# Packed first loads and a by-token last projection in a float32 decoder trunk

## Chip, core and metric
One NeuronCore of one Trainium2 chip runs the whole program in one launch. The metric is device time in microseconds (us) of one execution; the runs shown are separate executions of the same program. Engines are named as in the profile: PE (TensorE), PEld (its weight loads), DVE (VectorE), ACT (ScalarE), POOL (GpSimd), SP (the engine that issues most transfers).

## The reference, cut to what matters
A trunk of two pre-norm layers on x of shape (1, 256, 1024), all float32: `h = h + mixer(rmsnorm(h))`, `h = h + conv_ffn(rmsnorm(h))`, twice, then a final norm.

```python
z = h @ w_in                       # conv_ffn: 1024 -> 2 * 2816
u, g = z[..., :D_FF], z[..., D_FF:]
a = causal_dwconv(u, conv_w) + conv_b
return (silu(a) * g) @ w_out       # 2816 -> 1024
...
return rmsnorm(h, final_norm_g)    # h * rsqrt(mean(h * h) + 1e-6) * g
```

The mixer of layer 0 starts with one input projection `hn @ w_in` of 2048 columns, cut by channel into a double-gated convolution and a pooling path. Layer 1 has attention heads instead.

## The kernel before, in words
P is 128, T is 256 tokens, D is 1024, and NK = 8 chunks of 128 channels. The residual `h` lives in SBUF by channel: `h[128, 8, 256]`. Every matmul operand is split into a high and a low float32r part, and every product is three matmuls (`mm3`, L272 to L275): high by high, high by low, low by high. Weights stream from memory in blocks of 128 x 1024 floats (rows of 4 KB; 512 KB a block). A block is loaded on SP's queue (L139), ACT casts it to its high part (L131), DVE subtracts to get the low part (L132), and up to six blocks are prepared ahead (`ahead`). The order of PE's instructions is the program order; the other engines are ordered by a scheduler, except in the stretches under `manual_schedule`, where ACT and DVE too keep the program order.

The start (L242 to L269): the first unit of layer 0 needs all of `h` and four blocks of weights (two of kind x, two of kind y). They come in five steps of chunks, (0,1), (1,2), (2,4), (4,6), (6,8). Each step issues three transfers on SP: its chunks of `h` (L252) and the matching columns of one x block and one y block (L254). Rows are 1 KB for the first two steps and 2 KB for the others. The norm's weights `vec[:, :8]` come by POOL's queue (L171). Then, step by step, ACT and DVE scale `h` by the norm weights and split it (`hgh`, `hgl`, L194 and L195) and cut the weights. PE runs 12 matmuls per chunk, 96 in all (L434 to L438). The token norm's factor is applied later, to rows of the results (`rrow`), so that the projection need not wait for it.

Layer 0's mixer goes on by units: pooling and convolution of a unit run on DVE, POOL and ACT while PE projects the next units; `even_add` then adds their output products, and `yb` (L394) is the pooling path's split input to them.

The MLP (`ffn`, L483): for each of 22 channel blocks f, an input step of 48 matmuls of 256 columns (`z`), and four blocks later an output step of 24 matmuls of 256 columns. `Acc` (L311) holds the output by channel: eight accumulators of 128 channels x 256 tokens in four PSUM banks. The weights are the stationary operand (128 x 128) and the hidden values `y` of 256 tokens the moving one. The last two blocks' products are kept as `tail`, and `close` (L329) runs them bank by bank and adds the residual on DVE (L337).

The end (`final`, L768): after the last MLP, `h` is by channel and the final norm is by token. So PE turns `h` in 16 transposes of 128 x 128 (L781), two per chunk, between the `close` steps and after the last; ACT sums the squares (L786); DVE works out the variance of both token blocks together, POOL raises it to the power of -0.5 (L806), and ACT and DVE scale the output (L810, L812), which leaves in five transfers on SP's queue (L811, L813).

Of the kernel before, what the change touches and what calls it, by code (L numbers as in the profile page):

```python
# [18 lines left out]
P = 128  # L19
# [21 lines left out]
LOOK = 6  # L41

# columns of the packed per-channel vectors
# [5 lines left out]
def trunk(ctx, tc, a, out):  # L49
# [35 lines left out]
    for j in range(NG):  # L85
        even_in_blocks(j)
        if j >= 2:
            even_out_blocks(j - 2)
# [82 lines left out]
    nc.gpsimd.dma_start(vec[:, :NK], a["vec"][:, :NK])  # L171
# [29 lines left out]
    class Stats:  # L201
        """The mean square of h per token, and from it the norm's factor, by column and by row."""
# [4 lines left out]
        def feed(self, b):  # L207
            """Squares of h's chunks 2b, 2b+1."""
# [38 lines left out]
    def step_parts(k0, k1):  # L247
        s, e = (k0 % 4) * 256, (k0 % 4 + k1 - k0) * 256
        return [(i, s, e) for i in (k0 // 4, 2 + k0 // 4)]
# [5 lines left out]
    for i in range(4):  # L255
        done[blocks[i][0]] = first[i][1:]
# [9 lines left out]
    state["next"] = 4  # L266
    ahead(6)
    nc.sync.dma_start(vec[:, NK:], a["vec"][:, NK:])
    nc.sync.dma_start(rc, a["rcnt"])  # L269

# [6 lines left out]
    def in_chunk(o, w, hg, between=None):  # L277
        """o[f, t] = sum_k w[k, f] hg[k, t]; between() comes halfway."""
# [6 lines left out]
    def in_pair(z, at, hg, between=None):  # L285
        """Two chunks that share a bank, in step; at(k, c) gives the weights of chunk c's rows k."""
# [7 lines left out]
    def split(pool_, src, scale, name, bufs=None, between=None):  # L294
        """src (SBUF or PSUM) times a per-partition scale, as two float32r parts."""
# [15 lines left out]
    class Acc:  # L311
        """Eight [128, 256] accumulators over four PSUM banks."""
# [15 lines left out]

    def close(acc, tail, b, between=None):  # L329
        """The last products of an output projection's bank b, and the residual."""  # L330
# [5 lines left out]
        hb = h[:, 2 * b:2 * b + 2, :]  # L336
        nc.vector.tensor_add(hb, acc.t[b], hb)  # L337

    def boundary(acc, tail, g0):
        """The end of an output projection, and the next layer's input."""  # L340
# [11 lines left out]
    # causal convolution over time, width 3, on the free axis: t = the newest tap, then the two before it  # L352
# [11 lines left out]

    with tc.tile_pool(name="ev", bufs=2) as ev, tc.tile_pool(name="evc", bufs=1) as evc:
# [5 lines left out]
        def pool_sums(j, z):  # L371
            """Trailing sums, by doubling."""
# [7 lines left out]
        def pool_less(j):  # L380
            """Trailing mean less the token."""
# [50 lines left out]
        w0 = [[weights(("e" + kind, 0, q)) for q in range(2)] for kind in "xy"]  # L432
        zx0, zy0 = (psA.tile([P, 2, T], F32, tag="ps", name="z" + kind) for kind in "xy")
        for k in range(NK):  # L434
            for c in range(4):
                wh, wl = (x[:, (k % 4) * 256 + (c % 2) * P:][:, :P] for x in w0[c // 2][k // 4])
                mm3((zx0, zy0)[c // 2][:, c % 2, :], wh, wl, hg[0][:, k, :], hg[1][:, k, :],
                    k == 0 and c % 2 == 0, k == NK - 1, skip=True)  # L438
        ahead()
# [40 lines left out]
        st, hg = boundary(acc, tail, V_FFN)  # L480

# [1 line left out]
    def ffn(l, st, hg, ps_z, ps_acc, end, aside=None):  # L483
        with tc.tile_pool(name=f"ff{l}", bufs=2) as fp:
            acc = Acc(ps_acc)
# [16 lines left out]
            for kind, f in ffn_steps:  # L502
                if kind == "out":
                    acc.add_all(weights(("fo", l, f)), ready.pop(f))
# [26 lines left out]
    # T5 bias along each query row, negated, with the causal mask beyond it  # L531
# [15 lines left out]
    st, hg = ffn(0, st, hg, psA, psB, lambda acc, tail: boundary(acc, tail, V_MIX + NK), t5_rows)  # L547

# [1 line left out]
    with tc.tile_pool(name="od", bufs=2) as od, tc.tile_pool(name="odc", bufs=1) as odc:  # L550
# [4 lines left out]
        def values(n):  # L555
            """Values by token, 512 channels."""
# [19 lines left out]
        # forget gates  # L576
# [34 lines left out]
        def pair_bias(p):  # L611
            """Forget sums of a FoX pair's keys, or the T5 biases of a MoBA pair's queries."""
# [276 lines left out]
```

## Time and profile before

| what | value |
|---|---|
| device time, three runs | 590.21, 590.57, 592.21 us; median 590.57 |
| profiled execution, first to last instruction (span) | 588.8 us |
| profiled execution's own device time | not listed apart from its span |
| PE busy | 575.7 us, 98% |
| DVE busy | 429.9 us, 73% |
| ACT busy | 324.9 us, 55% |
| POOL busy | 78.9 us, 13% |
| bytes moved by transfers | 106.07 MB, mean 180 GB/s |

The busy time of PE counts overlapping matmuls, whose ends are modelled; the pace of PE is read from the distance between starts. An engine's idle time matters only where the others wait for it.

### The profile page before, as it was taken

To read this page: it belongs to the slowest core of one execution; us is meant where nothing else is said; L and a number is where in the kernel's file an instruction comes from. 1 tells how busy PE (TensorE), PEld (TensorE's weight loads), DVE (VectorE), ACT (ScalarE), POOL (GpSimd) and SP (SyncE) were. 2 spreads that over 40 slices of the span, in tenths; PEclk is the share of its full clock that TensorE was granted. 3 is DMA by queue.
4 is the path that set the end of the run, shared out by engine and by line. 5 is a ranking of instruction groups with operands and counts; after the bars stand their busy time and mean duration, and the time that the engine had idled before them with its cause. 6 is when DMAs were issued, how large, how long until landed. Compare 5 with 4: busy or idle time off the path is not lost.

```text
span 588.8 us, 11640 instructions
## 1 busy us (share of the span) xinstructions
PE 575.7 (98%) x4664; PEld 562.8 (96%) x4664; DVE 429.9 (73%) x700; ACT 324.9 (55%) x538; POOL 78.9 (13%) x91
## 2 busy tenths in 40 slices
PE   8999999999999999999999999999999999999993
PEld 6999999999999999998898999999999999999993
DVE  5899687876568677668678888498767677766733
ACT  6764476554355454447577777476554444545412
POOL 1441231000000000004162164031000000000000
PEclk9999999999999999999999999999999999999997
DMA  8975726656687555653675534347555555554001
GB/s 250 401 269 190 241 81 245 215 171 132 151 320 235 184 189 185 188 180 129 215 218 178 162 127 145 126 143 249 187 190 184 185 187 180 180 181 141 1 1 71
DMA packets 31941, 106.07 MB, mean 180 GB/s; under 512 B 4256, under 2 KB 5416, under 8 KB 31888
## 3 DMA queue, kind: packets, MB, share of 16 engines
q1 hardware_dynamic: 30240, 101.09, 50.8%
q0 software_dynamic: 1648, 4.25, 4.2%
q8 instruction: 36, 0.59, 0.4%
q14 instruction: 17, 0.14, 0.1%
HBM read 102.69 MB, written 2.63 MB: 179 GB/s over the span
## 4 chain that ended last, share of the span: by engine, by line
PE 60%; issue 32%; DVE 4%; ACT 1%; DMA 1%; POOL 0%; SPq 0%; POOLq 0%; ACTq 0%
PE z L274 8%; PE z L273 7%; PE z L275 7%; PE acc L273 6%; PE acc L274 6%; PE acc L275 6%; PE zk L273 1%; DVE lo L132 1%; PE zq L273 1%; PE pv L565 1%; PE zk L274 1%; PE zk L275 1%; PE pv L567 1%; PE pv L566 1%; PE zq L274 1%
## 5 line engine op out<-in xcount | busy, mean ns | idle before, releaser
L132 DVE TENSOR_TENSOR lo<-st,hi 128x1024 fp32r<-128x1024 f32 (+2 forms) x196 | 235.3, 1210 | 85.1 <-ACT hi L131 84.9
L131 ACT CAST hi<-st 128x1024 fp32r<-128x1024 f32 (+2 forms) x196 | 196.7, 1012 | 154.6 <-PE z L274 62.3
L274 PE MATMUL z<-hgl,hi 128*128 128x256 f32 x704 | 199.6, 284 | 0.1
L273 PE MATMUL z<-hgh,hi 128*128 128x256 f32 x704 | 199.7, 284 | 0.0
L275 PE MATMUL z<-hgh,lo 128*128 128x256 f32 x704 | 199.5, 283 | 0.0
L274 PEld LDWEIGHTS z<-hgl,hi 128*128 128x128 f32 x704 | 135.0, 192 | 0.5 <-DVE hgl L195 0.5
L275 PEld LDWEIGHTS z<-hgh,lo 128*128 128x128 f32 x704 | 135.0, 192 | 0.0
L273 PEld LDWEIGHTS z<-hgh,hi 128*128 128x128 f32 x704 | 135.0, 192 | 0.0
L273 PE MATMUL acc<-y_h,hi 128*128 128x256 f32 x352 | 99.7, 283 | 0.0
L274 PE MATMUL acc<-y_l,hi 128*128 128x256 f32 x352 | 99.2, 282 | 0.0
L275 PE MATMUL acc<-y_h,lo 128*128 128x256 f32 x352 | 99.2, 282 | 0.0
L273 PEld LDWEIGHTS acc<-y_h,hi 128*128 128x128 f32 x352 | 66.5, 189 | 0.4 <-issue 0.4
L274 PEld LDWEIGHTS acc<-y_l,hi 128*128 128x128 f32 x352 | 66.4, 189 | 0.0
L275 PEld LDWEIGHTS acc<-y_h,lo 128*128 128x128 f32 x352 | 66.3, 188 | 0.0
L492 DVE TENSOR_TENSOR zs<-z,rrow 128x512 f32<-128x512 f32 x44 | 30.2, 690 | 19.9 <-PE z L275 19.7
L300 ACT CAST y_h<-y 128x256 fp32r<-128x256 f32 x44 | 17.9, 406 | 47.9 <-DVE y L499 47.9
L357 ACT ACTIVATE t<-zs,vec 128x256 f32<-128x256 f32 x44 | 26.3, 598 | 9.2 <-DVE zs L492 9.2
L306 DVE TENSOR_TENSOR y_l<-y,y_h 128x256 fp32r<-128x256 f32 x44 | 18.7, 424 | 16.5 <-ACT y_h L300 16.5
L215 POOL TENSOR_TENSOR sqs<-sq 128x512 f32<-128x512 f32 x4 | 5.2, 1295 | 186.4 <-ACT sq L210 161.9
L195 DVE SCALAR_TENSOR_TENSOR hgl<-h,vec,hgh 128x256 fp32r<-128x256 f32 x32 | 22.3, 735 | 6.8 <-ACT hgh L194 6.8
L806 POOL TENSOR_TENSOR rcol<-var,mhalf 128x2 f32<-128x2 f32 x1 | 0.7, 689 | 182.2 <-DVE var L804 182.2
L361 DVE SCALAR_TENSOR_TENSOR t<-zs,vec,t 128x254 f32<-128x254 f32 x44 | 21.2, 483 | 1.5
(197 smaller groups left out, 1002.6 us busy)
## 6 DMA issues: line engine op xcount, KB each, us to landing
st<-in_ff_in SPq DMA_DIRECT2D x88, 512.0 KB, 3.7
st<-in_ff_out SPq DMA_DIRECT2D x44, 512.0 KB, 3.3
st<-in_od_qk SPq DMA_DIRECT2D x16, 512.0 KB, 4.6
st<-in_ev_in SPq DMA_DIRECT2D x10, 512.0 KB, 7.7
st<-in_ev_out SPq DMA_DIRECT2D x8, 512.0 KB, 4.5
st<-in_od_v SPq DMA_DIRECT2D x8, 512.0 KB, 4.2
st<-in_od_out SPq DMA_DIRECT2D x8, 512.0 KB, 4.0
st<-in_ev_in SPq DMA_DIRECT2D x10, 256.0 KB, 5.5
```

The source lines that it names most:

```text
L131: nc.scalar.copy(hi[:, s:e], st[:, s:e])
L132: nc.vector.tensor_sub(lo[:, s:e], st[:, s:e], hi.bitcast(F32)[:, s:e])
L195: nc.vector.scalar_tensor_tensor(hg[1][:, k, :], h[:, k, :], g, hg[0].bitcast(F32)[:, k, :], op0=ALU.mult, op1=ALU.subtract)
L273: nc.tensor.matmul(o, wh, xh, start=start, stop=False, skip_group_check=skip)
L274: nc.tensor.matmul(o, wh, xl, start=False, stop=False, skip_group_check=skip)
L275: nc.tensor.matmul(o, wl, xh, start=False, stop=stop, skip_group_check=skip)
L300: nc.scalar.copy(hi, src)
L306: nc.vector.tensor_sub(lo, src, hi.bitcast(F32))
L357: nc.scalar.activation(t, u, AF.Identity, scale=col(w0 + 2), bias=bias)
L361: nc.vector.scalar_tensor_tensor(t[:, 2:], u[:, :T - 2], col(w0), t[:, 2:], op0=ALU.mult, op1=ALU.add)
L492: nc.vector.tensor_mul(zs, z, rrow[:, None, :].to_broadcast([P, 2, T]))
L565: nc.tensor.matmul(pv[i], xh, wh, start=k == 0, stop=False)
```

## The change
Two edits go together.

The start. The host lays the first unit's inputs out in one array `first` of 8 x 128 rows of 776 floats (3104 bytes): the norm weight of the row's channel, seven floats of padding, 256 tokens of x, and 512 weights of the four projections. It is loaded in nine transfers on SP, one per chunk, with the first chunk's in two. The four blocks no longer use the staging buffers. POOL's load of the norm weights goes; `vec` comes whole, on SP, after six blocks of weights. ACT and DVE cut chunk by chunk, in program order; the first chunk's high part is copied by DVE. PE takes the first chunk's products in another order. Layer 0's residual is read from `first`, and `h` is written for the first time at the end of layer 0's mixer.

The end. In the last MLP a new `TokenAcc` holds the output by token: four banks of 128 tokens x 512 channels. At its creation, which is now at the first output step, 16 transposes put `h` into the banks, and the products add to it: `y` of 128 tokens is the stationary operand and 512 weights the moving one, 12 matmuls of 512 columns per output step. `final` then finishes block of tokens by block of tokens; there are no residual adds and no transposes in it. Each block's first half is stored from ACT's queue, the second from SP's.

```diff
-        piece = 512 if i < 6 else BLK
+        piece = 512 if i < 2 else BLK
...
-    nc.gpsimd.dma_start(vec[:, :NK], a["vec"][:, :NK])
...
-    first = [block_tiles(i) for i in range(4)]
-    steps = [(0, 1), (1, 2), (2, 4), (4, 6), (6, 8)]
...
-    for k0, k1 in steps:
-        nc.sync.dma_start(h[:, k0:k1, :], a["xt"][:, k0:k1, :])
-        for i, s, e in step_parts(k0, k1):
-            nc.sync.dma_start(first[i][0][:, s:e], blocks[i][1][:, s:e])
+    first = fst.tile([P, NK, FIRST], F32, name="first")
+    w0h, w0l = ([wgt.tile([P, 2, 512], F32R, tag=t, name=f"{t}{m}_0") for m in range(4)] for t in ("hi", "lo"))
+    x0 = first[:, :, LEAD:LEAD + T]
+    w0 = first[:, :, LEAD + T:]
+    resid = {"t": x0}
+    for k in range(NK):
+        for s, e in ((0, LEAD + T), (LEAD + T, FIRST)) if k == 0 else ((0, FIRST),):
+            nc.sync.dma_start(first[:, k, s:e], a["first"][k, :, s:e])
     st = Stats()
     with tc.manual_schedule(engines={mybir.EngineType.Activation, mybir.EngineType.DVE}):
-        for k0, k1 in steps:
-            for k in range(k0, k1):
-                scaled_chunk(hg, k, V_MIX)
-            for i, s, e in step_parts(k0, k1):
-                cut(*first[i], s, e)
+        for k in range(NK):
+            g = first[:, k, 0:1]
+            nc.scalar.activation(hg[0][:, k, :], x0[:, k, :], AF.Copy, scale=g)
+            wh, wl = (t[k // 2][:, k % 2, :] for t in (w0h, w0l))
+            if k == 0:
+                nc.vector.tensor_copy(wh, w0[:, k, :])
+            else:
+                nc.scalar.copy(wh, w0[:, k, :])
+            nc.vector.scalar_tensor_tensor(hg[1][:, k, :], x0[:, k, :], g, hg[0].bitcast(F32)[:, k, :],
+                                           op0=ALU.mult, op1=ALU.subtract)
+            nc.vector.tensor_sub(wl, w0[:, k, :], w0h[k // 2].bitcast(F32)[:, k % 2, :])
         for b in range(4):
-            st.feed(b)
+            st.feed(b, x0)
     ahead(6)
-    nc.sync.dma_start(vec[:, NK:], a["vec"][:, NK:])
+    nc.sync.dma_start(vec, a["vec"])
...
+    class TokenAcc:
+        def __init__(self, ps):
+            self.t = [[ps.tile([P, 512], F32, tag="ps", name=f"ta{i}{n}") for n in range(2)] for i in range(2)]
+            for k in range(NK):
+                for i in range(2):
+                    nc.tensor.matmul(self.t[i][k // 4][:, (k % 4) * P:(k % 4 + 1) * P], h[:, k, i * P:(i + 1) * P],
+                                     ident, is_transpose=True, start=k % 4 == 0, stop=False, skip_group_check=True)
+
+        def add(self, i, n, w, y, last):
+            s = slice(n * 512, (n + 1) * 512)
+            yh, yl = (x[:, i * P:(i + 1) * P] for x in y)
+            mm3(self.t[i][n], yh, yl, w[0][:, s], w[1][:, s], False, last, skip=True)
...
+            products = [(w, x, c) for c in range(4) for w, x in ((w0h, 0), (w0h, 1), (w0l, 0))]
+            if k == 0:
+                products = [(w, x, c) for w, x in ((w0h, 0), (w0h, 1), (w0l, 0)) for c in range(4)]
...
             for i in range(2):
-                r = rcol[:, i:i + 1]
-                for lo, hi in ((0, 256), (256, 512)) if i == 0 else ((0, 512),):
-                    nc.scalar.activation(o[:, i, lo:hi], hg_[:, i, lo:hi], AF.Copy, scale=r)
-                    nc.sync.dma_start(out[i, :, lo:hi], o[:, i, lo:hi])
-                nc.vector.scalar_tensor_tensor(o[:, i, 512:], pt[i][1], r, gb[:, 512:], op0=ALU.mult, op1=ALU.mult)
+                r, v = rcol[:, i:i + 1], var[:, i:i + 1]
+                for n in range(2):
+                    for m, (w, y) in enumerate(tail):
+                        acc.add(i, n, w, y, m == len(tail) - 1)
+                    nc.scalar.activation(junk, acc.t[i][n], AF.Square, accum_out=sums[:, i, n:n + 1])
+                    if n == 0:
+                        nc.vector.tensor_mul(hg_[:, i, :], acc.t[i][0], gb[:, :512])
+                        nc.vector.tensor_scalar(v, sums[:, i, 0:1], 1.0 / D, EPS, op0=ALU.mult, op1=ALU.add)
+                nc.vector.scalar_tensor_tensor(v, sums[:, i, 1:2], 1.0 / D, v, op0=ALU.mult, op1=ALU.add)
+                nc.gpsimd.tensor_tensor(r, v, mhalf[:, 0:1], op=ALU.pow)
+                nc.vector.scalar_tensor_tensor(o[:, i, 512:], acc.t[i][1], r, gb[:, 512:], op0=ALU.mult, op1=ALU.mult)
+                nc.scalar.activation(o[:, i, :512], hg_[:, i, :], AF.Copy, scale=r)
+                nc.scalar.dma_start(out[i, :, :512], o[:, i, :512])
                 nc.sync.dma_start(out[i, :, 512:], o[:, i, 512:])
...
-    ffn(1, st, hg, psB, psA, ordered_final)
+    ffn(1, st, hg, psB, psA, TokenAcc, ordered_final)
```

## Rows read from the trace of the kernel before

**Rows 1.** The page's first part: busy time and share of the span.
```profile
span 588.8 us, 11640 instructions
PE 575.7 (98%) x4664; PEld 562.8 (96%) x4664; DVE 429.9 (73%) x700; ACT 324.9 (55%) x538; POOL 78.9 (13%) x91
```
**Rows 2.** Waits of PE, whole span: who waited for whom, total us, times, longest.
```profile
PE zx L273 <- ACT hi L131: 1.4, 1, 1.4
PE fin L781 <- DVE h L337: 0.9, 1, 0.9
PE acc L274 <- DVE ybl L308: 0.8, 1, 0.8
```
**Rows 3.** Windows of the start: length, PE, PEld, DVE, ACT, POOL busy, PEclk, DMA share, GB/s.
```profile
2.00:5.00 3.00, 3.00 (x8) 1.88 (x7) 0.40 (x1) 1.16 (x5) 1.21 (x4) 1.00 0.92 244
5.00:11.00 6.00, 4.36 (x28) 3.90 (x29) 3.79 (x10) 3.67 (x9) 0.00 (x0) 1.00 0.90 240
11.00:16.00 5.00, 5.00 (x44) 5.00 (x43) 4.45 (x9) 4.95 (x11) 0.15 (x1) 1.00 1.05 396
16.00:33.00 17.00, 17.00 (x144) 17.00 (x143) 15.65 (x21) 12.99 (x18) 9.62 (x9) 1.00 1.03 403
```
**Rows 4.** Timeline of the start: start, us, engine, line, op, out<-in [idle before <-releaser].
```profile
0.73 0.39 SPq L252 DMA_DIRECT2D h<-in_xt  x1
...
4.06 0.51 ACT L194 ACTIVATE hgh<-h,vec 128x256 fp32r<-128x256 f32 x1 [1.83 <-DMA vec<-in_vec]
...
4.91 0.58 PE L273 MATMUL zx<-hgh,hi 128*128 128x256 f32 x1
...
8.38 0.91 ACT L194 ACTIVATE hgh<-h,vec 128x256 fp32r<-128x256 f32 x2 [2.14 <-DMA h<-in_xt]
...
9.93 0.39 PE L273 MATMUL zx<-hgh,hi 128*128 128x256 f32 x1 [1.42 <-ACT hi L131]
...
14.18 1.29 DVE L132 TENSOR_TENSOR lo<-st,hi 128x512 fp32r<-128x512 f32 x2
...
19.16 0.28 PE L273 MATMUL zx<-hgh,hi 128*128 128x256 f32 x1
```
**Rows 5.** DMA issues of the first 30 us: size of each, median us to landing.
```profile
h<-in_xt SPq DMA_DIRECT2D x2, 128.0 KB, 2.6
```
**Rows 6.** DVE after the first unit (timeline), and the window of the first mixer.
```profile
16.30 1.99 DVE L132 TENSOR_TENSOR lo<-st,hi 128x512 fp32r<-128x512 f32 x2 [0.83 <-ACT hi L131]
...
26.00:66.00 40.00, 39.16 (x328) 38.96 (x327) 37.56 (x68) 21.65 (x31) 9.94 (x11) 1.00 0.72 254
```
**Rows 7.** Window of the last MLP, columns as in the windows above.
```profile
440.00:575.00 135.00, 135.00 (x1132) 135.00 (x1132) 87.77 (x120) 61.71 (x88) 0.00 (x0) 1.00 0.41 137
```
**Rows 8.** Timeline of one output step: its first product, and the next input step's.
```profile
503.31 0.28 PE L273 MATMUL acc<-y_h,hi 128*128 128x256 f32 x1
...
506.16 0.28 PE L273 MATMUL z<-hgh,hi 128*128 128x256 f32 x1
```
**Rows 9.** Timeline of layer 1's second values: first product, and what follows them.
```profile
290.99 0.40 PE L565 MATMUL pv<-hi,hgh 128*128 128x512 f32 x1
...
301.90 0.28 PE L273 MATMUL zq<-hgh,hi 128*128 128x256 f32 x1
```
**Rows 10.** Timeline of the end, from the first tail product to the last store.
```profile
572.10 0.28 PE L273 MATMUL acc<-y_h,hi 128*128 128x256 f32 x1
...
574.95 0.60 PE L781 MATMUL fin<-ident,h 128*128 128x128 f32 x4
...
576.80 0.60 PE L781 MATMUL fin<-ident,h 128*128 128x128 f32 x4
...
577.33 0.60 ACT L786 ACTIVATE junk<-fin 128x512 f32<-128x512 f32 x1 [9.80 <-PE fin L781]
...
581.82 0.69 POOL L806 TENSOR_TENSOR rcol<-var,mhalf 128x2 f32<-128x2 f32 x1 [182.18 <-DVE var L804]
...
582.54 1.41 DVE L812 SCALAR_TENSOR_TENSOR o<-fin,rcol,gb 128x512 f32<-128x512 f32 x2 [0.81 <-POOL rcol L806]
...
584.98 0.40 SPq L813 DMA_DIRECT2D out<-o  x1
```

More of the change, by code (lines that the diff above doesn't have):

```diff
@@ L41 @@
 LOOK = 6
+LEAD = 8
+FIRST = LEAD + T + 512
 V_MIX, V_FFN, V_FIN, V_EC, V_PS, V_FC, V_FB = 0, 16, 32, 40, 52, 56, 188
@@ L83, in even_out_blocks @@
         block(("eo", j + NG), a["ev_out"][GROUPS[j] + NG])
-    for j in range(NG):
+    for j in range(1, NG):
         even_in_blocks(j)
@@ L327, in add_all @@
                 self.add(dc, w, y, False)
+    class TokenAcc:
[9 more added lines that the diff above has]
+            mm3(self.t[i][n], yh, yl, w[0][:, s], w[1][:, s], False, last, skip=True)
+        def add_all(self, w, y):
+            for i in range(2):
+                for n in range(2):
+                    self.add(i, n, w, y, False)
     def close(acc, tail, b, between=None):
@@ L430, in even_in @@
             return z
-        w0 = [[weights(("e" + kind, 0, q)) for q in range(2)] for kind in "xy"]
         zx0, zy0 = (psA.tile([P, 2, T], F32, tag="ps", name="z" + kind) for kind in "xy")
         for k in range(NK):
[L435 to L439, printed above, removed]
+            products = [(w, x, c) for c in range(4) for w, x in ((w0h, 0), (w0h, 1), (w0l, 0))]
+            if k == 0:
+                products = [(w, x, c) for w, x in ((w0h, 0), (w0h, 1), (w0l, 0)) for c in range(4)]
+            for n, (w, x, c) in enumerate(products):
+                nc.tensor.matmul((zx0, zy0)[c // 2][:, c % 2, :], w[k // 2][:, k % 2, c * P:(c + 1) * P], hg[x][:, k, :],
+                                 start=k == 0 and w is w0h and x == 0 and c % 2 == 0,
+                                 stop=k == NK - 1 and w is w0l, skip_group_check=True)
         pwb = small_block(evc, a["ev_pw"], "pw")
@@ L480, in trunk, with ffn @@
         st, hg = boundary(acc, tail, V_FFN)
-    def ffn(l, st, hg, ps_z, ps_acc, end, aside=None):
+    resid["t"] = h
+    fs.close()
+    def ffn(l, st, hg, ps_z, ps_acc, kind_acc, end, aside=None):
         with tc.tile_pool(name=f"ff{l}", bufs=2) as fp:
-            acc = Acc(ps_acc)
+            acc = None
             ready = {}
@@ L771, in final @@
             nc.gpsimd.dma_start(gb, bass.AP(tensor=gsrc.tensor, offset=gsrc.offset, ap=[[0, P], [1, D]]))
-            pt = [[psB.tile([P, 512], F32, tag="ps", name=f"fin{i}{n}") for n in range(2)] for i in range(2)]
-            sums = fin.tile([P, 3, 2], F32, name="sums")
-            junk = fin.tile([P, 2, 512], F32, name="junk")
+            sums = fin.tile([P, 2, 2], F32, name="sums")
+            junk = fin.tile([P, 512], F32, name="junk")
             hg_ = fin.tile([P, 2, 512], F32, name="hg_")
@@ L776, in final @@
             o = fin.tile([P, 2, D], F32, name="o")
-            def turned(b):
-                for k in (2 * b, 2 * b + 1):
-                    for i in range(2):
-                        nc.tensor.transpose(pt[i][k // 4][:, (k % 4) * P:(k % 4 + 1) * P],
-                                            h[:, k, i * P:(i + 1) * P], ident)
-            def squares(n, lo, hi, part):
-                for i in range(2):
-                    nc.scalar.activation(junk[:, i, lo:hi], pt[i][n][:, lo:hi], AF.Square,
-                                         accum_out=sums[:, part, i:i + 1])
@@ L789, in final @@
-            close(acc, tail, 0)
-            close(acc, tail, 1)
-            turned(0)
-            close(acc, tail, 2)
-            turned(1)
-            squares(0, 0, 512, 0)
-            close(acc, tail, 3, between=lambda: turned(2))
-            squares(1, 0, 256, 1)
-            turned(3)
-            for i in range(2):
-                nc.vector.tensor_mul(hg_[:, i, :], pt[i][0], gb[:, :512])
-            var = fin.tile([P, 2], F32, name="var")
-            nc.vector.tensor_add(var, sums[:, 0, :], sums[:, 1, :])
@@ L802, in final @@
-            nc.vector.tensor_scalar(var, var, 1.0 / D, EPS, op0=ALU.mult, op1=ALU.add)
-            squares(1, 256, 512, 2)
-            nc.vector.scalar_tensor_tensor(var, sums[:, 2, :], 1.0 / D, var, op0=ALU.mult, op1=ALU.add)
-            rcol = fin.tile([P, 2], F32, name="rcol")
-            nc.gpsimd.tensor_tensor(rcol, var, mhalf, op=ALU.pow)
-            for i in range(2):
-                r = rcol[:, i:i + 1]
-                for lo, hi in ((0, 256), (256, 512)) if i == 0 else ((0, 512),):
-                    nc.scalar.activation(o[:, i, lo:hi], hg_[:, i, lo:hi], AF.Copy, scale=r)
-                    nc.sync.dma_start(out[i, :, lo:hi], o[:, i, lo:hi])
-                nc.vector.scalar_tensor_tensor(o[:, i, 512:], pt[i][1], r, gb[:, 512:], op0=ALU.mult, op1=ALU.mult)
+            var = fin.tile([P, 2], F32, name="var")
@@ new lines, in final @@
+            rcol = fin.tile([P, 2], F32, name="rcol")
+            for i in range(2):
+                r, v = rcol[:, i:i + 1], var[:, i:i + 1]
+                for n in range(2):
+                    for m, (w, y) in enumerate(tail):
[9 more added lines that the diff above has]
+                nc.scalar.dma_start(out[i, :, :512], o[:, i, :512])
```

24 lines of the change are left out of this document (13 added, 11 removed).

## The prediction, made before the change was run

> **What bounds the kernel now.** I read the page's busy times first: PE is busy for 98% of the span [rows 1]. Then PE's waits, since only these and the pace of its products can be shortened: they are few, 1.4 us at the start for weights, 0.8 us in layer 0's mixer for `ybl`, 0.9 us at the end for `h` [rows 2]. So the kernel is bound by PE's pace between two edges, and the change works at both edges and on the pace.
>
> At the start the reader should see loads that come too slowly. 240 to 244 GB/s move until 11 us, about 400 after it [rows 3]. PE's first product starts at 4.91, a hole of 1.42 us ends at 9.93, and the 96 products of the first unit end where the next unit begins, 19.16 [rows 4]. At the pace of 0.119 us that rows 8 show (24 products from 503.31 to 506.16) they need 11.4 us, so 2.8 us are lost.
>
> At the end, the first tail product starts at 572.10 [rows 10] and the span ends at 588.8 [rows 1]: 16.7 us, of which 48 products are 5.7.
>
> The span is my base. The median of the runs, 590.57, lies 1.8 us above it; I take that as what lies around the span and leave it as it is.
>
> **Part by part: the output products of the last MLP.** Twenty output steps of 24 products with 256 columns become 20 of 12 with 512. A step now takes 506.16 - 503.31 = 2.85 us [rows 8]. The trace has the new form already: layer 1's values are products of 128x128 by 512 columns, 48 of them in 301.90 - 290.99 = 10.91 us, 0.2273 each [rows 9]. Twelve are 2.73 us. The step saves 0.12 us, twenty save 2.4. PE has no gap in this stretch (135.00 of 135.00 us busy) and DVE only 87.77 [rows 7], so nothing else hides the gain or takes it over. Bounds: 0, if a wide product took exactly two narrow ones, and 2.4.
>
> The cause is a share of each product that does not grow with its columns: twice 0.1188 less 0.2273 is 0.0103 us. The Trainium skill (TensorE: Matmul & The Clock Gate, section "Wait - 56ns, not 53.3ns?") puts the fixed cost of a warm product at about 2.5 ns; by that the term would be 240 x 2.5 ns = 0.6 us. The rows show four times that, so the measured pair decides.
>
> **The transposes.** Sixteen stood at the end, 12 of them between products. Now all stand at the first output step, in PE's stream, with nothing to wait for (`h` and the banks were ready long before). From one group of four to the next it is 576.80 - 574.95 = 1.85 us, less 12 products of 0.119 leaves 0.42 for four [rows 10]. Sixteen cost 1.7 us. Bounds 1.4 to 2.4.
>
> **The tail.** Let T be the first tail product. The 24 wide products need 5.46 us, and block 0's norm runs beside block 1's products. ACT sets the new end, since it works in program order. Its second square of block 0 starts at 12 x 0.2273 + 0.2 = T+2.9; a square with its sum takes 0.7 (rounded up from the 0.60 of [rows 10] for the read of the sum), DVE's variance 0.2, the power 0.69 with 0.1 of handover, ACT's scaling 0.7 (the rate of DVE's, 1.41 for two), its store's issue 0.4 [rows 10]. So ACT is free at T+5.8 only. Queued behind it are both squares of block 1, whose products ended at T+4.3 and T+5.6: they end at T+7.2. Then variance 0.2, power 0.8, DVE's scaling 0.75: the last stores issue at T+8.9. From the last issue to the end of the span it took 588.8 - 584.98 = 3.8 us [rows 1, 10]; now two stores leave together, so I add 0.15. The tail is 12.9 instead of 16.7: 3.8 us saved. Bounds: 4.6 if ACT's store does not hold it up, 2.8 if each handover is 0.1 longer and the two stores go one after the other. The four residual adds, which the last transposes waited for, go with it.
>
> **The start.** A chunk is 776 x 4 x 128 bytes = 0.397 MB, the total is as before. The first 128 KB landed 2.6 us after an issue at 0.73, at 3.3 [rows 4, 5]; ACT's first scaling waited for `vec` until 4.06 and no longer does. But PE's first product needs 512 cut weights: 0.26 MB more at 244 GB/s is 4.4, and DVE's copy at most what a subtraction of that size takes, 0.65 (two in 1.29 [rows 4]): 5.0, as before. Chunk 0 and 1 are through at about 8.5 (the low parts come last), and six chunks of 12 products follow at 1.44 us: 17.1 at best, 2.1 us sooner.
>
> What the loads do decides more. No row shows rows of 3104 bytes. The nearest in time are those before 11 us (240 GB/s), the nearest in size those of 2 and 4 KB after it (396 to 403) [rows 3]. Since 2 KB rows stand in both stretches, row length alone cannot be the cause of the slow start. At 240 until 11 us chunk 4 lands at 10.7, its low part is cut at 12.4, and the unit ends at 17.9: PE gains 1.3, by order alone. DVE however ends the unit's cuts then at 15.7, against 14.18 + 1.29 = 15.5 now. And DVE is the next bound: 37.56 of 40 us busy in the mixer [rows 6], and PE already waits for its `ybl` [rows 2]. What PE gains beyond DVE's lead is given back there. At 400, DVE is through at 13.9, 1.6 sooner, and may also save the 0.83 us in which it waited for ACT [rows 6]. So the start brings 0 to 2.1. I take 1.2, a rate between the two.
>
> The Trainium skill (DMA: Bandwidth & Descriptors, section "Specifications") has transfers at line rate from 512 bytes on. By that the 1 and 2 KB rows had nothing to gain from length, and the start would bring 0. The trace agrees in part: 2 KB rows do reach 396 GB/s.
>
> The load of `vec` by POOL goes, and `vec` whole stands on SP behind six blocks; it is due in the mixer's convolutions, after 30 us, and 6.4 MB at 400 GB/s are in by about 18. The other moved steps cost nothing: blocks 0 to 5 are those that were loaded next anyway, and the residual read from another tile is the same DVE add.
>
> **The sum.** -2.4 + 1.7 - 3.8 - 1.2 = -5.7: span 583.1, time 584.9.
>
> **The rivals.**
> 1. *The loads are no faster, and the start gives its gain back at `ybl`* (that this half of the change does not do what it says). For it: the rate before 11 us did not depend on row length. Against: PE's hole at 9.93 goes in any case. Without the 1.2: 586.1. The line-rate rule of the Trainium skill (DMA: Bandwidth & Descriptors) comes out here too.
> 2. *Wide products are two narrow ones*, so that the output steps save nothing: 584.9 + 2.4 = 587.3. Against it stand 48 products in [rows 9]; for it only that those stood in another stage. By the fixed cost that the Trainium skill gives (TensorE: Matmul & The Clock Gate) it would be 586.7, with 0.6 saved in place of 2.4.
> 3. *Both*, or the tail keeps only 2.8 and the start nothing and the products half: 588.5, or within 0.3% of before.
> 4. *Slower*: the packed chunks load badly. All of a chunk must land before any of it is used, and its rows are not multiples of 512 bytes. The place is the first unit. The price: with chunks at r GB/s the unit ends near 2 + 3180/r + 3.4 us. The gain elsewhere is 4.5, so the total is slower by over 1.8 us once the unit ends after 25.5, that is below some 160 GB/s; at half of the 240, 120 GB/s, it ends at 31.9 and the time is 586.1 + 12.7 = 598.8. For it: nothing in the rows. Against: every rate in [rows 3].
>
> **How the numbers follow.** Forecast 0.53, rival 1 0.25, rival 2 0.08, rival 3 and the like 0.09, slower 0.05. A measurement of this kernel can tell about 0.3%, 1.8 us, from no change. Faster by more are the forecast and rivals 1 and 2: 0.86; same 0.09; slower 0.05. The range goes from the full start gain and a quick tail (584.9 - 0.9 - 0.8 = 583.2) to beyond rival 2 (588.0), which leaves out most of rivals 3 and 4 and some of each end.
>
> **What would show it.** Products of 512 columns in the last MLP 0.227 us apart; sixteen transposes in one row before the first; DVE without residual adds at the end; ACT's squares of block 1 behind its own store; from first tail product to the end of the span about 13 us; the second unit's first product near 17 us, and the GB/s before 11 us. The prediction is wrong if PE's wait for `ybl` grows by all that the first unit gained, if output steps stay at 2.85 us, or if another wait stands ahead of the last stores.

## The result, and the profile after

The changed kernel takes 585.81 us (median of 4 runs, 585.67 to 586.32) against 590.58 for the kernel before (4 runs beside it): a ratio of 0.9915, 95% interval 0.9901 to 0.9929. That is 4.77 us less, where 5.7 were forecast. The profiled execution has a span of 584.0 and a time of 585.75.

The page's first lines, which answer to [rows 1], show the same kind of kernel, bound by PE at 98%, with 264 products fewer:

```profile
span 584.0 us, 11086 instructions
...
PE 573.6 (98%) x4400; PEld 549.7 (94%) x4400; DVE 428.1 (73%) x696; ACT 324.5 (56%) x530; POOL 79.1 (14%) x91
```

PE's waits (who for whom, total us, times, longest) answer to [rows 2]. The 1.4 for weights and the 0.9 for `h` are gone, the 0.8 for `ybl` stands, and a wait that nobody had forecast is new, for `rcol`:

```profile
PE acc L277 <- DVE ybl L311: 0.8, 1, 0.8
PE pst L230 <- POOL rcol L240: 0.6, 1, 0.6
```

**The start.** Windows of the start, columns as in [rows 3]: the last number, GB/s, is 279 and 372 where 244 and 240 stood.

```profile
2.00:5.00 3.00, 3.00 (x9) 2.24 (x9) 0.99 (x3) 0.73 (x3) 0.18 (x1) 1.00 1.00 279
5.00:11.00 6.00, 5.86 (x43) 5.53 (x43) 4.89 (x10) 4.70 (x10) 0.00 (x0) 1.00 0.99 372
11.00:16.00 5.00, 5.00 (x44) 5.00 (x43) 4.19 (x8) 4.62 (x10) 1.29 (x1) 1.00 1.04 403
```

The timeline of the start, against [rows 4]: SP issues its nine loads in 4.42 us, the first product starts 0.3 us sooner, DVE's last cut of the unit ends at 14.06 (before: 14.18 + 1.29 = 15.47), and the second unit begins at 17.40 where it began at 19.16. PE leads by 1.76 us.

```profile
0.73 4.42 SPq L254 DMA_DIRECT2D first<-in_first  x9
...
4.59 0.81 PE L462 MATMUL zx<-hgh,hi 128*128 128x256 f32 x2
...
13.38 0.68 DVE L267 TENSOR_TENSOR lo<-first,hi 128x512 fp32r<-128x512 f32 x1
...
17.40 0.28 PE L276 MATMUL zx<-hgh,hi 128*128 128x256 f32 x1
```

**Where a part of the lead goes.** It is kept through layer 0's mixer and lost in part behind it, where the MLP's norm is made. `pst` is first the sum over the channels and then the factor by rows. Before the change they came at these times (timelines of POOL and PE, the kernel before; the first line is the first of POOL's four memsets of layer 1's key tiles `kz`):

```profile
69.97 0.53 POOL L643 MEMSET kz<- 64x512 f32 x1
...
88.67 0.51 PE L223 MATMUL pst<-ones,tot 128*128 128x1 f32 x4
...
91.99 0.42 PE L229 MATMUL pst<-ident,rcol 128*128 128x128 f32 x2
```

and after it (timelines of POOL, DVE and PE of the changed kernel, put in order of time):

```profile
80.28 0.53 POOL L672 MEMSET kz<- 64x512 f32 x1
...
82.40 3.46 DVE L134 TENSOR_TENSOR lo<-st,hi 128x1024 fp32r<-128x1024 f32 x2
...
85.21 1.24 POOL L221 TENSOR_TENSOR tot<-sqs 128x256 f32<-128x256 f32 x1
...
86.46 2.34 DVE L134 TENSOR_TENSOR lo<-st,hi 128x1024 fp32r<-128x1024 f32 x2
...
86.53 0.58 PE L224 MATMUL pst<-ones,tot 128*128 128x1 f32 x4
...
88.73 0.14 DVE L238 TENSOR_SCALAR var<-pst 128x2 f32<-128x2 f32 x1
...
88.95 1.65 POOL L240 TENSOR_TENSOR rcol<-var,mhalf 128x2 f32<-128x2 f32 x1 [0.76 <-DVE var L238]
...
90.66 0.43 PE L230 MATMUL pst<-ident,rcol 128*128 128x128 f32 x2 [0.57 <-POOL rcol L240]
```

The first `pst` is 2.14 us sooner, the second 1.33: PE arrives, and `rcol` is not there. The four memsets of `kz` are new in this stretch (POOL did them at 69.97 to 72.18 before). `first` holds 24,832 bytes a partition until layer 0's mixer ends. So tiles that stood above it moved up, into the place that `kz` takes later; the memsets now wait for them, and fall between POOL's sums of squares. Those then stand beside DVE's cuts, and `var` queues behind the cuts. Two cuts took 3.46 us next to the sums and 2.34 behind them.

**The output steps.** First product of one step and of the input step behind it, against [rows 8]: 2.77 us instead of 2.85. Forecast were 2.73.

```profile
443.22 0.39 PE L276 MATMUL ta<-hi,y_h 128*128 128x512 f32 x1
...
445.99 0.28 PE L276 MATMUL z<-hgh,hi 128*128 128x256 f32 x1
```

The first step, with the sixteen transposes, begins at 415.88 and ends at 420.42: 4.54 us, so 1.77 for the transposes.

**The end.** Timeline from the first tail product, against [rows 10]:

```profile
570.95 0.39 PE L276 MATMUL ta<-hi,y_h 128*128 128x512 f32 x1
...
574.00 0.60 ACT L813 ACTIVATE junk<-ta 128x512 f32<-128x512 f32 x1 [0.77 <-PE ta L278]
...
575.55 0.73 ACT L820 ACTIVATE o<-hg__7141,rcol 128x512 f32<-128x512 f32 x1 [0.86 <-POOL rcol L818]
...
576.30 0.40 ACTq L821 DMA_DIRECT2D out<-o  x1
...
576.76 0.60 ACT L813 ACTIVATE junk<-ta 128x512 f32<-128x512 f32 x1 [0.48 <-PE ta L278]
...
577.48 0.60 ACT L813 ACTIVATE junk<-ta 128x512 f32<-128x512 f32 x1
...
578.58 0.55 POOL L818 TENSOR_TENSOR rcol<-var,mhalf 128x1 f32<-128x1 f32 x1 [3.06 <-DVE var L817]
...
579.92 0.36 ACTq L821 DMA_DIRECT2D out<-o  x1
```

From 570.95 to the end of the span are 13.05 us; 16.7 before. ACT takes block 0's scaling and its store's issue (575.55 to 576.70) ahead of block 1's squares. The row names PE as what it waited for, but those products had ended near 575.4.

The lead in order: 1.76 at the second unit, 1.33 behind layer 0's mixer, 1.36 at the first output step (417.24 before, 415.88 after), 1.15 at the first tail product (the transposes cost a little more than the wide products bring), 1.15 + 3.61 = 4.76 at the end. The spans differ by 4.8.

### The profile page after: what moved, and what is told of

It reads as the page before. It is cut to its first block, busy times and chain, and to the rows that moved or that the text cites. A ratio compares the mean times of both kernels' runs of the same rounds, so it can differ in the third digit from the quotient of the medians.

```text
span 584.0 us, 11086 instructions
## 1 busy us (share of the span) xinstructions
PE 573.6 (98%) x4400; PEld 549.7 (94%) x4400; DVE 428.1 (73%) x696; ACT 324.5 (56%) x530; POOL 79.1 (14%) x91
## 4 chain that ended last, share of the span: by engine, by line
PE 93%; DVE 4%; issue 1%; DMA 1%; ACT 0%; POOL 0%; SPq 0%; POOLq 0%; ACTq 0%
PE z L277 14%; PE z L276 14%; PE z L278 14%; PE acc L276 6%; PE acc L277 6%; PE acc L278 6%; PE ta L278 3%; PE ta L277 3%; PE ta L276 3%; PE zk L276 1%; PE zq L276 1%; PE pv L594 1%; PE zk L277 1%; PE zk L278 1%; PE pv L595 1%; PE pv L596 1%
## 5 line engine op out<-in xcount | busy, mean ns | idle before, releaser
L134 DVE TENSOR_TENSOR lo<-st,hi 128x1024 fp32r<-128x1024 f32 (+1 forms) x186 | 230.4, 1246 | 86.0 <-ACT hi L133 85.3
L133 ACT CAST hi<-st 128x1024 fp32r<-128x1024 f32 (+1 forms) x186 | 191.7, 1039 | 153.8 <-PE z L277 63.1
L276 PE MATMUL acc<-y_h,hi 128*128 128x256 f32 x176 | 49.7, 283 | 0.0
L277 PE MATMUL acc<-y_l,hi 128*128 128x256 f32 x176 | 49.5, 282 | 0.0
L278 PE MATMUL acc<-y_h,lo 128*128 128x256 f32 x176 | 49.5, 281 | 0.0
L278 PE MATMUL ta<-hi,y_l 128*128 128x512 f32 x88 | 34.7, 394 | 0.0
L276 PE MATMUL ta<-hi,y_h 128*128 128x512 f32 x88 | 34.7, 394 | 0.0
L277 PE MATMUL ta<-lo,y_h 128*128 128x512 f32 x88 | 34.6, 393 | 0.0
L276 PEld LDWEIGHTS acc<-y_h,hi 128*128 128x128 f32 x176 | 33.2, 189 | 0.4 <-issue 0.4
L277 PEld LDWEIGHTS acc<-y_l,hi 128*128 128x128 f32 x176 | 33.2, 188 | 0.0
```

What stands on the lines that cost most here:

```text
L133: nc.scalar.copy(hi[:, s:e], st[:, s:e])
L134: nc.vector.tensor_sub(lo[:, s:e], st[:, s:e], hi.bitcast(F32)[:, s:e])
L276: nc.tensor.matmul(o, wh, xh, start=start, stop=False, skip_group_check=skip)
L277: nc.tensor.matmul(o, wh, xl, start=False, stop=False, skip_group_check=skip)
L278: nc.tensor.matmul(o, wl, xh, start=False, stop=stop, skip_group_check=skip)
```

## The experiments

**1 and 2. Each half alone.** `start_only` is the changed kernel with the old end, `end_only` the changed kernel with the old start.

```diff
-    ffn(1, st, hg, psB, psA, TokenAcc, ordered_final)
+    ffn(1, st, hg, psB, psA, Acc, ordered_final)
...
```

> The packed first loads alone, the end as before. Theory: the first unit ends near 17.4 us as in the changed kernel (19.2 before), the lead of 1.75 us holds to the end of layer 0's mixer, 0.4 of it is lost at the boundary behind it, and nothing later touches it: 1.3 to 1.4 us below the kernel before, 589.2. Rival (the two halves help each other): the start alone gives under 0.7 or over 2 us.

> The last output projection and the norm by token alone, the start as before. Theory: 20 output steps of 2.77 us for 2.85, 1.8 us of transposes, and a tail of 13.05 for 16.7: 3.4 to 3.5 us below the kernel before, 587.1. Rival (the tail is shorter only because PE came earlier): under 2.5 us.

Measured: 589.49 us for the start alone (ratio 0.9967, 0.9952 to 0.9983) and 587.41 for the end alone (0.9944, 0.9925 to 0.9964), against 590.74: -1.25 and -3.33. They add up to -4.58, nearly the -4.77 of both. As far as intervals of about 1 us to either side can tell, the halves are separate: neither gives or takes much from the other.

The old start costs more than its hole in some executions. In the profiled executions of `end_only` and of `pad_before` (below), both with the old loads, PE first waited through the hole of [rows 4] (1.23 and 1.45 us there), and then TensorE's granted clock fell. Their windows from 11 to 16 us, columns as in [rows 3]:

```profile
11.00:16.00 5.00, 5.00 (x30) 4.86 (x29) 4.34 (x9) 4.96 (x11) 0.00 (x0) 0.66 1.05 393
11.00:16.00 5.00, 5.00 (x31) 5.00 (x31) 4.67 (x9) 4.87 (x10) 0.00 (x0) 0.66 1.05 398
```

For some 3 us of it the clock stands at 0.50, the level of 1.2 GHz, and a product takes 0.213 us instead of 0.119; some 15 products lose about 1.4 us. The profiled execution of the kernel before had the same hole and kept 1.00. But of the 24 executions of that kernel that ran beside these, 14 took 590.06 to 590.79 us at a mean clock of 0.994 to 0.996, and 10 took 591.86 to 594.92 at 0.990 to 0.994; all 11 of `start_only` lie between 588.86 and 589.91, and in no trace with packed loads does the clock fall in the first 40 us. So the packed loads seem to take away this loss too, which a difference of medians shows only in part. That the ten are such falls at the start, no trace shows.

**3. The place of a tile alone.** `pad_before` is the kernel before with a tile of `first`'s size that nothing reads, freed where `first` is.

```diff
+    fst = fs.enter_context(tc.tile_pool(name="fst", bufs=1))
+    pad = fst.tile([P, NK, 776], F32, name="pad")
...
+    fs.close()
```

> The kernel before with nothing but an unused tile of 24832 bytes a partition, held where the packed array is held in the changed kernel, from the start to the end of layer 0's mixer. Theory: it pushes the pooling tiles onto the place of layer 1's key tiles, so that POOL's four clearings of those come only between the sums of squares at the end of the mixer; they slow DVE there, the norm's variance comes later, and PE waits 0.4 to 0.7 us for the factor: 0.3 to 0.7 us above the kernel before. Rival (the 0.4 us are lost because PE comes earlier): no wait of PE for the factor, time as before within 0.1 us.

Measured: 591.35 (ratio 1.0007, 0.9994 to 1.0021), which settles nothing: 6 of its 11 executions lie at 590.55 to 591.35, 5 at 592.09 to 593.39, two groups as in the kernel before. The trace does (timeline of PE): the 0.6 us wait for `rcol` is there, and the two `pst` are 4.09 us apart instead of 3.32.

```profile
89.74 0.56 PE L223 MATMUL pst<-ones,tot 128*128 128x1 f32 x4
...
93.83 0.43 PE L229 MATMUL pst<-ident,rcol 128*128 128x128 f32 x2 [0.56 <-POOL rcol L239]
```

From the first of the mixer's last 96 products to the second `pst` it takes 24.11 us; the kernel before takes 23.73 and the changed one 24.14. So a tile that nobody uses costs 0.4 us, and PE's earlier arrival is not needed for it.

**4. The memsets out of the way.** `const_kz` is the changed kernel with `kz` among the constants, zeroed at the start (and 7 staging buffers instead of 8, for the room).

```diff
-STAGED = 8
+STAGED = 7
...
+    kzs = [const.tile([P, 2, 2, T], F32R, name=f"kz{i}") for i in range(2)]
...
-        kzs = [odc.tile([P, 2, 2, T], F32R, name=f"kz{i}") for i in range(2)]
```

> The changed kernel with layer 1's key tiles in a place of their own, cleared at the start, and 7 staging buffers for 8 to make room. Theory: POOL adds the squares without a break, the wait of 0.6 us for the norm's factor in the first MLP goes, and the time is 0.3 to 0.7 us below the changed kernel, 585.3. Rival (PE comes earlier, DVE's cuts are in the way): the wait stays and the time is that of the changed kernel within 0.1 us; if the missing buffer matters, above it.

Measured: 585.98 (0.9914, 0.9895 to 0.9934), no gain that this can tell. Its timeline of DVE and PE in the same stretch:

```profile
83.77 2.89 DVE L134 TENSOR_TENSOR lo<-st,hi 128x1024 fp32r<-128x1024 f32 x2
...
87.49 0.50 PE L228 MATMUL pst<-ones,tot 128*128 128x1 f32 x4
...
90.92 0.43 PE L234 MATMUL pst<-ident,rcol 128*128 128x128 f32 x2
```

The wait is gone, and the stretch takes 23.85 us: of the 0.4 lost, 0.3 come back. In the profiled execution they are used up by a first unit that ended 0.55 us later; between two medians of four runs each that scatter by 0.7, 0.3 us can't be told. The expectation was too high.

**5. ACT's order at the end.** `tail_order` puts block 0's scaling behind block 1's first square, and its store on SP.

```diff
+            def first_half(i):
+                nc.scalar.activation(o[:, i, :512], hg_[:, i, :], AF.Copy, scale=rcol[:, i:i + 1])
+                (nc.scalar if i else nc.sync).dma_start(out[i, :, :512], o[:, i, :512])
...
+                        if i == 1:
+                            first_half(0)
...
-                nc.scalar.activation(o[:, i, :512], hg_[:, i, :], AF.Copy, scale=r)
-                nc.scalar.dma_start(out[i, :, :512], o[:, i, :512])
...
+                if i == 1:
+                    first_half(1)
```

> The changed kernel, but at the end block 0's scaling of its first half stands on ACT behind block 1's first square instead of ahead of it, and its store leaves from SP instead of ACT. Theory (ACT's program order sets the end of the tail): block 1's first square starts when its products end, about 4.4 us after the first tail product instead of 5.8, the second about 0.7 us sooner than in the changed kernel, and all behind it comes 0.7 us sooner: tail 12.3 to 12.4 us instead of 13.05, time 585.1. Rival (the last products and the handovers set the end, ACT's hold is slack): the tail stays at 13.0 us, time 585.8.

Its timeline of ACT, with the first tail product at 571.13:

```profile
575.56 0.60 ACT L817 ACTIVATE junk<-ta 128x512 f32<-128x512 f32 x1 [0.70 <-PE ta L278]
...
576.15 0.71 ACT L809 ACTIVATE o<-hg__7141,rcol 128x512 f32<-128x512 f32 x1
576.96 0.60 ACT L817 ACTIVATE junk<-ta 128x512 f32<-128x512 f32 x1
...
579.26 0.40 ACTq L810 DMA_DIRECT2D out<-o  x1
```

Measured: 585.44 (0.9896, 0.9871 to 0.9922). The first square starts 4.43 us behind the first tail product instead of 5.81, and the tail is 583.3 - 571.13 = 12.17 instead of 13.05. So ACT's program order set the end, as the prediction had it. The span of this execution moved by 0.7, since it came to the tail 0.18 us later; the median of the five (585.02 to 585.83) moved by 0.4, which their scatter leaves open.

**6. Both repairs.** `tail_const` joins 4 and 5.

> The changed kernel with two edits together: layer 1's key tiles lie in the pool of constants and are zeroed at the start (so that nothing of POOL's stands between the sums of squares behind layer 0's mixer), and at the end block 0's scaling stands behind block 1's first square. If both losses are real and separate: the 0.6 us wait for rcol is gone, the tail is 0.7 us shorter, time 584.7 to 585.0. If the key tiles' gain is given back at the wait for ybl, as the run of that edit alone left open: only the tail counts, 585.1 to 585.3.

Measured: 584.52 us (4 runs, 584.42 to 584.59; ratio 0.9881, 0.9853 to 0.9909), span 582.8. Against the changed kernel that is 1.2 of the span: 0.9 in the tail (12.17 again) and 0.3 in the lead at the first tail product. It beats both kernels.

**7 to 9. Why the loads are faster.** Three kernels change one thing of the packed loads each: `rows776` the length of the rows, `two_loads` the number of transfers, `stride8k` the distance of the rows in memory. The lines of the diff stand in this order.

```diff
+                nc.sync.dma_start(first[:, k, :].rearrange("p (q f) -> p q f", q=4),
+                                  a["first4"][k - 1].rearrange("q p f -> p q f"))
...
-        for s, e in ((0, LEAD + T), (LEAD + T, FIRST)) if k == 0 else ((0, FIRST),):
+        for s, e in (0, LEAD + T), (LEAD + T, FIRST):
...
-    f = np.zeros((NK, P, FIRST), np.float32)
+    f = np.zeros((NK, P, 2048), np.float32)
```

> The changed kernel, but chunks 1 to 7 of the packed array lie in memory in four pieces, so that a partition's part of a chunk is four rows of 776 bytes instead of one of 3104; number, order and size of the transfers are the same. Theory A (the loads became faster because of the long rows): GB/s from 5 to 11 us falls from 372 toward the 240 of before, the first unit ends near 19 instead of 17.4, time 586.8 to 587.4. Theory B (they became faster because few transfers read one stretch of memory each): the rate stays at 370 and the time at 585.8.

> The changed kernel, but every chunk of the packed array comes in two transfers (132 KB with the residual, 256 KB of weights), 16 in all instead of nine, near the 15 of the kernel before; the memory that is read and its order are the same. Theory A (the loads became faster because there are fewer transfers): GB/s from 5 to 11 us falls toward the 240 of before (below 300), the first unit ends after 18.5 us, time above 586.8. Theory B (the number of transfers does not matter): 360 to 380 GB/s, the first unit ends at 17.4 to 17.9, time 585.8. Both ways the first half of a chunk lands earlier than the whole did, which may be worth some tenths to ACT.

> The changed kernel, but in memory the rows of 3104 bytes of the packed array stand 8192 bytes apart, as the rows of the kernel before did, instead of one right behind the other; number and size of the transfers are the same. Theory A (the loads became faster because a transfer reads one unbroken stretch of memory): GB/s from 5 to 11 us falls toward the 240 of before (below 300), the first unit ends after 18.5 us, time above 586.8. Theory B (the place of the rows does not matter): 360 to 380 GB/s, first unit 17.4 to 17.9, time 585.8.

Windows of `rows776` (one line) and of `stride8k` (two), columns as above:

```profile
5.00:11.00 6.00, 5.55 (x41) 5.14 (x41) 4.79 (x9) 4.25 (x9) 0.00 (x0) 1.00 1.10 339
```

```profile
2.00:5.00 3.00, 2.96 (x7) 1.80 (x6) 0.00 (x0) 0.72 (x3) 0.18 (x1) 1.00 0.74 163
5.00:11.00 6.00, 4.86 (x26) 4.89 (x27) 5.26 (x11) 4.18 (x9) 0.00 (x0) 1.00 1.03 389
```

Short rows: 339 GB/s, 586.88 us. The first unit ends at 17.60, only 0.2 later, but DVE's last cut ends at 14.97 instead of 14.06. PE then loses 0.35 in the second unit, where the norm's factor comes late from DVE and POOL, and waits 0.13 longer for `ybl`. Neither theory fits whole: most of the rate stays (B), yet the time is A's, and it is lost through DVE. Rows far apart: 163 GB/s up to 5 us, 389 behind it; the first unit ends at 19.49, the time is 587.06 (586.41 to 587.74). Theory A has the time right, but the slow stretch is another one than the 5 to 11 us of the kernel before. Two transfers a chunk: 353 GB/s, and the first unit ends at 17.45, as theory B says; but the time is 588.59. That loss of 2.8 us neither theory had. Timeline of SP and DVE of `two_loads`:

```profile
0.73 7.97 SPq L254 DMA_DIRECT2D first<-in_first  x16
...
27.35 0.43 DVE L471 TENSOR_TENSOR rrow<-rrow 128x256 f32<-128x256 f32 x1 [1.28 <-ACT rrow L233]
...
46.64 0.48 DVE L311 SCALAR_TENSOR_TENSOR ybl<-zp,vec,ybh 128x256 fp32r<-128x256 f32 x1
```

SP issues until 8.7 us instead of 5.15, and the next units' blocks stand behind it on the queue. ACT waits 1.57 us for one at 21.4, DVE runs out of cuts and stands idle for 1.28 us, `ybl` comes at 46.64 instead of 45.24, and PE waits 2.2 us for it, 1.4 more than in the changed kernel. That is half of the loss. The other half is the clock; two windows of `two_loads`, the wait and what follows it:

```profile
45.00:47.10 2.10, 0.00 (x0) 0.00 (x0) 1.83 (x7) 1.49 (x3) 0.00 (x0) 0.97 0.65 242
47.10:50.30 3.20, 3.13 (x14) 3.13 (x15) 3.20 (x7) 1.13 (x3) 0.00 (x0) 0.50 0.18 51
```

Behind the wait the granted clock stands at 0.50, the level of 1.2 GHz, until 50.3, and 15 products take 0.213 us each instead of 0.119: 1.4 us. The shorter waits for `ybl` of the other kernels (0.8 to 1.5 us) had no such fall behind them. One of the six executions took 586.85, at the highest mean clock (0.997; the others 0.994 and 0.995), as if it had been spared the fall; no trace shows that.

What the new order of ACT's, DVE's and PE's work in the first unit is worth without the new loads, no run shows. No single one of the three explains the 240 of [rows 3]; that cause stays open.

**10. The pace of the wide products: banks.** `bank_each` lets the bank change at every product.

```diff
-                for n in range(2):
-                    self.add(i, n, w, y, False)
+                yh, yl = (x[:, i * P:(i + 1) * P] for x in y)
+                for l, r in ((yh, w[0]), (yh, w[1]), (yl, w[0])):
+                    for n in range(2):
+                        nc.tensor.matmul(self.t[i][n], l, r[:, n * 512:(n + 1) * 512], start=False, stop=False,
+                                         skip_group_check=True)
```

> The changed kernel, but the twelve wide products of an output step take turns between the two banks of a token block, so that the bank changes at every product instead of at every third, and the stationary changes at every second product only. Theory A (the 0.2315 us of a wide product, where layer 1's values take 0.2273, come from changing banks): the pace gets worse, 0.24 and more, and the time rises by 2 us or more (240 products by 0.009) to 588. Theory B (they come from loading the stationary): half of them need no new one and the pace falls to 0.227 or below, the time by 1 us to 584.8. Theory C (neither): pace 0.231, 585.8.

Measured: 586.09 us, steps of 2.77 to 2.78 us: theory C. Changing banks costs nothing. PE's weight loads number 4400, one for each product as before, so that the order saved no load, and theory B was not put to the test.

**11 and 12. The pace: operands and their place.** `pace_probe` changes the operands of the twenty steps in turn; `y_near` moves `y` next to `hgh`.

```diff
+            if c % 4 == 1:
+                y = [x[:, c % NK, :] for x in hg]
+            if c % 4 == 3:
+                w = [x[:, 0:4, :].rearrange("p k t -> p (k t)") for x in hg]
...
+            if c % 4 == 2:
+                self.t = [t[0], t[0]]
```

```diff
+    ypl = pool("ypl", LAG + 2)
     hgp = pool("hgp", 1)
...
-                ready[f] = split(fp, y, None, "y_", bufs=LAG + 2)
+                ready[f] = split(ypl if l else fp, y, None, "y_", bufs=LAG + 2)
```

> The changed kernel, but of the twenty wide output steps of the last MLP only each fourth does its own products; each second of four takes a chunk of the MLP's input (hgh, hgl) as stationary operand in place of y, each third adds both token blocks into the two banks of the first, each fourth takes four chunks of the MLP's input as moving operand in place of the weights. The output projection is thus not the reference's; the number and size of the products are. Layer 1's values take 0.2267 us a product, with hgh as stationary and two banks. Theory A (the place of the stationary costs the 0.005): steps with hgh as stationary fall to 2.72 us, the others stay at 2.77. Theory B (four banks): the steps with two banks fall to 2.72. Theory C (the place of the moving operand): the steps with another moving operand do. Theory D (none of these; the first products behind a stage of 256 columns are slow everywhere, and twelve do not get past them): all stay at 2.77.

> The changed kernel, but in the last MLP the split hidden values y lie in their own 12 KB a partition, directly below hgh and hgl (addresses 105 to 117 thousand instead of 155 to 168 thousand); the room comes from three staging buffers (5 instead of 8), so the time as a whole may rise for late weights and is not the point. Theory A (what kept the probe's products with y slow and those with hgh quick is the place of the stationary operand): the wide output steps take 2.75 us as with hgh, and the long run of 60 products settles near 0.227 us each, 13.5 instead of 13.7 us. Theory B (it is something else about y, say that it was written shortly before): steps stay at 2.77 and the 60 products at 0.232 each.

One step of `pace_probe` with `hgh` as stationary, then one of `y_near` (timelines of PE, first product and the next input step's):

```profile
426.37 0.40 PE L276 MATMUL ta<-hi,hgh 128*128 128x512 f32 x1
...
429.12 0.28 PE L276 MATMUL z<-hgh,hi 128*128 128x256 f32 x1
```

```profile
426.66 0.40 PE L277 MATMUL ta<-hi,y_h 128*128 128x512 f32 x1
...
429.41 0.28 PE L277 MATMUL z<-hgh,hi 128*128 128x256 f32 x1
```

Both take 2.75 us. The probe's steps with two banks, with another moving operand, or with nothing changed take 2.77 to 2.78. In `y_near` all steps but the first take 2.75, and the last 60 products, which run without a break from 562.66 to the last start at 576.06, take 13.40 us; in the changed kernel 13.70 (562.59 to 576.29). From one start to the next it is 0.233, 0.236, 0.228, 0.233, 0.231 and then 0.2267 on and on; with `y` in its old place it goes on between 0.228 and 0.241, 0.232 in the mean. So the stationary operand's place sets the pace. (`y_near` also moves the weights, the moving operand, 12 thousand bytes down, but the probe found no effect of that operand's place.) Why, no run shows. The time of `y_near`, 585.60 in a single run, is not compared: with 5 staging buffers PE's wait for `ybl` is 1.5 us.

## Why the prediction was right, and where not

The sum was -2.4 + 1.7 - 3.8 - 1.2 = -5.7. Measured it is -1.6 + 1.8 - 3.6 - 1.4 = -4.8. The direction and the range held, and the forecast was 0.9 too low. That the start's 1.4 comes so near the 1.2 is luck: 1.76 were gained, more than taken, and 0.4 of them lost behind layer 0's mixer, which nothing in the prediction foresaw.

**Output products, the term that was mis-sized.** The step "Twelve are 2.73 us" took the mean of 48 products in another stage [rows 9]. A step is 2.77, so twenty save 1.6. The 0.04 have two halves: the first five products behind a stage of 256 columns are slow wherever the operands lie (2.747 for twelve at best), and `y` lies in a slower place than `hgh` (0.027 a step). The first was to be read before the change: in the stretch of [rows 9] the first five intervals are 0.228 to 0.236 and the others 0.225 to 0.228. The second was not, since no product there has `y` as stationary. Rival 2, wide products like two narrow ones, falls. The step saved 6.7 ns for each product start that went (0.08 us by twelve), where the Trainium skill (TensorE: Matmul & The Clock Gate, "Wait - 56ns, not 53.3ns?") has 2.5 ns; the operands also changed roles, so the 6.7 are not the cost of a start alone.

**Transposes.** 1.7 forecast, 1.77 measured.

**The tail** went by the prediction's own steps: ACT free at T + 5.8 (576.70, that is T + 5.75), block 1's squares done at T + 7.2 (578.17), last stores issued at T + 8.9 (579.92, T + 8.97). From there 4.08 us instead of 3.95. `tail_order` shows that the hold on ACT, not the handovers, made the difference between the 3.6 saved and the upper bound of 4.6: without it 4.5 are saved.

**The start** brought 1.76 at the second unit, above the 1.2 taken and inside its bounds, because the loads were nearly as fast as at best. The argument that row length alone could not be the cause held in `rows776`. The argument that PE gives back at `ybl` what it gains beyond DVE's lead did not come out. DVE's last cut of the unit was 1.4 us sooner and PE's second unit 1.76, but the wait stayed at 0.84 us, since `ybl` itself started 1.75 us sooner (timelines of DVE, the kernel before and the changed one):

```profile
46.99 0.48 DVE L308 SCALAR_TENSOR_TENSOR ybl<-zp,vec,ybh 128x256 fp32r<-128x256 f32 x1
```

```profile
45.24 0.48 DVE L311 SCALAR_TENSOR_TENSOR ybl<-zp,vec,ybh 128x256 fp32r<-128x256 f32 x1
```

In both it starts 27.83 us behind the second unit's first product, and so it does in `stride8k` (19.49 and 47.31), where DVE's last cut was 0.9 sooner than before and PE's second unit 0.3 later. There `ybl` followed PE, not DVE's lead in the first unit. The wait grew only where blocks came late: by 0.13 us in `rows776`, 0.6 in `y_near` and 1.4 in `two_loads`. The argument had set the lower bound of 0, and so helped to put the 1.2 below the 1.76. Rival 1 falls with `start_only`, rival 4 with 279 GB/s in the first window. The Trainium skill's rule (DMA: Bandwidth & Descriptors, "Specifications") that 512 bytes are enough for line rate fits the small loss with 776 bytes, but not the conclusion drawn from it, that the start brings nothing.

**What the prediction did not have** is the place in memory. "The other moved steps cost nothing" counted instructions and queues, not that a tile held through a stage moves its neighbours. That cost 0.4 us, and `pad_before` shows it by itself. The memsets by themselves don't seem to slow DVE: a cut that overlapped the first of them by 0.4 us in the kernel before (69.11 to 70.34) took its usual 1.23; a longer overlap without the sums no trace has. What hurts is that they push POOL's sums beside the cuts (3.46 us for two instead of 2.34). That agrees, for the memsets as far as this short overlap goes, with the Trainium skill (SBUF — State Buffer, "Who interferes with whom"): a VectorE instruction with two inputs in SBUF contends with a GpSimd instruction that reads SBUF, not with one that only writes.

## What to carry to other kernels

Price a new form of a product from the steady part and the first few of a like stretch apart, and look where its stationary operand lies. When an edit holds a big tile longer, look at what else moves: work hoisted ahead of a stage waits for the old owner of its place and can fall into the worst stretch. And a lead at the start is kept only as far as the engine that is the next bound, here DVE, gets its blocks as early as PE. Look at the granted clock behind a long wait: the wait can cost twice its length.

## What was not expected of the hardware

- Products of 512 columns start every 0.2267 us with the stationary operand at 105 to 134 thousand in SBUF, and every 0.232 at 155 to 168 thousand; banks and the place of the moving operand change nothing.
- The first five such products behind a stage of 256 columns are 0.228 to 0.236 apart, in every place.
- An issue on SP's queue took about 0.5 us (16 in 7.97), so seven more transfers of the same bytes held up the weights behind them enough for PE to wait 1.4 us longer.
- Behind that wait of 2.2 us the granted clock stood at 0.50 for some 3 us, which cost another 1.4; behind a hole of 1.23 and of 1.45 us at the start it fell likewise, behind one of 1.42 it did not.
- Rows of 3104 bytes that lie 8192 bytes apart in memory came at 163 GB/s up to 5 us and at 389 behind it; without a gap between them at 279 and 372.
